# The order of ScalarE's two roundings in a down product, left to a planner or kept as written

## The chip, the cores and the metric

The kernel runs on one core of one Trainium2 chip. The metric is the device time of one execution in microseconds (us), the median of several runs. A profiled execution gives, beside its time, a record of every instruction on the core's engines: TensorE (PE for its matmuls, PEld for its weight loads), VectorE (DVE), ScalarE (ACT), GpSimd (POOL), SyncE (SP), and the DMA engines.

## The reference

One layer of an encoder on a sequence of 1024 frames of width 1024 in float32: a norm, a projection, two kinds of attention, gates and an output projection, then a feed-forward block of width 4096, and a last norm. The change touches the second matrix of the feed-forward block, `w_down`:

```python
h2 = rms_norm(x, norm2[l])
x = x + jnp.square(jax.nn.relu(h2 @ w_up[l])) @ w_down[l]
return rms_norm(x, final_norm)
```

## The kernel before, in words

All matrices are kept transposed, with features on the 128 partitions. A float32 product is made of three faster ones: each operand a is rounded to a_h (a type that TensorE reads at full rate), and a_l = a - a_h is rounded too; the product is w_h x_h + w_h x_l + w_l x_h. A rounding is a ScalarE copy (`CAST` in the profile), the subtraction runs on GpSimd for weights (`wl`) and on VectorE for activations (`xl`).

The large products go by a Strassen scheme: seven products of half size in place of eight. For the down product these are, in order, (weight, activation): (A11, B11), (S1, T1), (S2, T2), (S3, T3), (S4, B22), (A12, B21), (A22, T4). The activations B and T, 16 blocks of 128 x 512 for each product, were written to a DRAM array (`a_dram`) by the up product just before. The weights A are loaded from `wall`; the S are sums made on VectorE from blocks that stay in SBUF (`ka` and `ks`, 16 blocks each) and blocks that come in (`wr`, four buffers). S1 takes two loaded blocks a step, S3 one, S2 none, S4 one that is loaded into `ka`.

The stage has 7 x 16 = 112 steps. Step s takes one activation block and one weight block and issues 12 matmuls of 128 x 128 by 128 x 512: four output blocks m, three matmuls each. Four PSUM banks collect a product over its 16 steps; the other four are used by the next product. `prepare(s)` is written LEAD = 3 steps ahead of the matmuls of step s. It issues, in this order:

1. the load of the activation block (`xr`, six buffers);
2. its rounding `x..h` on ScalarE (line 1013; `xq` has XB = 4 buffers for each half);
3. the subtraction `x..l` on VectorE;
4. the loads and the VectorE sum of the weight of step s + WLEAD, that is two steps further on (`weight`, line 916);
5. the rounding `wh` of this step's own weight on ScalarE (line 165, in `split_w`; HL = 6 buffers), and the subtraction `wl` on GpSimd (line 167).

This written order is not by itself the order in an engine's queue. The program is laid out by a planner which simulates the kernel and puts, on each engine, an instruction ahead of another when it takes its inputs to be there sooner. `keep_in_program_order` takes that freedom from one instruction: it comes behind the instruction that was written last before it on the same engine, whatever that is, a DMA issue included. The class `Ordered` applies it to all calls made through it. Before the change the stage does so for VectorE's subtractions and sums (`VO`), for the loads on SyncE (`LO`) and for the last matmuls (`TO`); ScalarE and GpSimd are left to the planner, and so is all of `between`.

`between(n, banks)` takes a finished product out of PSUM, a piece after each step of the next product: a ScalarE copy after A11, VectorE totals after the others, after S2 and S3 also DMAs that add the residual from `x2_dram` (issued by GpSimd), and `final` (a square with its sum, and a scaling) for tiles that are complete. After S4 the norm of one half of the output is made and stored during A12, by `finish`: it stores in turn from SyncE and from ScalarE. The last product ends with the other half's norm. The other helpers are named in the profile's rows by line: L218 is the matmul of `product`, L96 any call through `Ordered`, L941 the residual's DMA, L233 and L948 the square and the scaling of `final`, L957 and L964 to L967 the norm and the stores of `finish`.

Of the kernel before, what the change touches and what calls it, by code (L numbers as in the profile page):

```python
# [82 lines left out]
def hybrid_block(ctx: ExitStack, tc: tile.TileContext, xT, g1, wall, wf, fb, relb, relt, rows, g2, g3, outT):  # L83
    nc = tc.nc
    V, A, G, T = nc.vector, nc.scalar, nc.gpsimd, nc.tensor
# [9 lines left out]
        def __getattr__(self, name):  # L95
            return lambda *a, **kw: tc.keep_in_program_order(getattr(self.eng, name)(*a, **kw))  # L96

    VO, TO, LO = Ordered(V), Ordered(T), Ordered(nc.sync)
    load_r = nc.gpsimd.dma_start

    def pool(stack, name, side, bufs=1, **kw):
# [10 lines left out]
    def tmp(name, dt=F32):  # L112
        return tp.tile([P, HALF], dt, tag="t", name=name, bufs=8)
# [9 lines left out]
    for n, (step, cm) in enumerate(((-1, 1), (1, -1))):  # L123
        m = cpool.tile([P, 3, P], F32R, tag=f"mask{n}", name=f"mask{n}")
        raw = tmp("raw")[:, 0:3 * P].rearrange("p (n q) -> p n q", q=P)
# [34 lines left out]
        load(q, wall[u, :, n, :])  # L160
        return q

    def split_w(src, name):
        wh = wp.tile([P, HALF], F32R, tag="wh", name=f"wh_{name}", bufs=HL)
        A.copy(wh, src)  # L165
        wl = wp.tile([P, HALF], F32R, tag="wl", name=f"wl_{name}", bufs=HL)
        G.tensor_tensor(wl, src, wh.bitcast(F32), op=ALU.subtract)  # L167
        return wh.rearrange("p (k m) -> p k m", m=P), wl.rearrange("p (k m) -> p k m", m=P)

    def plain_w(u, c):  # L170

        parts = [split_w(quarter(u, n), f"{u}_{n}") for n in ((0, 1), (3, 2))[c]]
        return [(parts[k // 4][0][:, k % 4, :], parts[k // 4][1][:, k % 4, :]) for k in range(KC)]

    def strassen_w(u, sum_eng, want=ALL):
# [20 lines left out]
        for name in want:  # L196
            if name in ("A11", "A12", "A22"):
                src = raw(int(name == "A12") + 2 * int(name == "A22"))
            elif name in ("S1", "S2"):
                if "S2" in want:  # L200
                    total("S2")
                src = total(name)
            elif name == "S3":
                src = raw(3)
                G.tensor_tensor(src, raw(0), src, op=ALU.subtract)
            else:
                src = total("S2")
                G.tensor_tensor(src, raw(1), src, op=ALU.subtract)
            out[name] = split_w(src, f"{u}_{name}")
# [102 lines left out]
    for h in range(2):  # L312
# [3 lines left out]
        for n, k in enumerate(PAIRED if h else range(KC)):  # L316
            xg = etile(f"xg{k}") if h == 0 else tmp(f"xg{k}")
            load(xg, xT[:, k, hs(h)])
            sum_squares(xg, n == 0, rstd[:, hs(h)], G if h else V)
            V.tensor_scalar(xg, xg, gt[:, 0, k:k + 1], None, op0=ALU.mult)  # L320
            split(xk(k, h), xg, V)
            blocks[k, h] = xg
            first, last = n == 0, n == KC - 1
            for c, ps in enumerate(banks):
                if (c, k // 4) not in ew:
                    ew[c, k // 4] = split_w(quarter(U_GATE + c // 2, ((0, 1), (3, 2))[c % 2][k // 4]), f"g{c}_{k}")
                w = [t[:, k % 4, :] for t in ew[c, k // 4]]
                for wi, xi in ((0, 0), (0, 1), (1, 0)):
                    T.matmul(ps, w[wi], xk(k, h)[xi], start=(first and wi + xi == 0), stop=(last and wi == 1),
                             skip_group_check=True)  # L330
            if h == 0 and first:
                for i, g in ((1, g2), (2, g3)):
                    load(gt[:, i, :], g)
                wr = tmp("wfr")[:, 0:KC * NH].rearrange("p (k m) -> p k m", m=NH)
                load(wr, wf)
                w40 = tmp("w40", F32R)[:, 0:KC * 40].rearrange("p (k m) -> p k m", m=40)
                V.memset(w40.bitcast(F32), 0.0)
                V.tensor_copy(w40[:, :, 0:NH], wr)
                V.tensor_tensor(w40[:, :, 32:40], wr, w40[:, :, 0:NH].bitcast(F32), op=ALU.subtract)
            for t in range(2):  # L340
                T.matmul(pf[0:40, :], w40[:, k, :], xk(k, h)[t], start=(first and t == 0), stop=(last and t == 1),
                         skip_group_check=True)
            if h == 1 and k >= 4:
                combine(k - 4, blocks[k - 4, 0], blocks[k - 4, 1], blocks[k, 0], blocks[k, 1], (V, G))
# [571 lines left out]
    def weight(n, k, vec, ld):  # L916

        u = U_DOWN + k
        if n in ("A11", "S4"):
            ld(hold("a", k), wall[u, :, int(n == "S4"), :])  # L920
        if n in ("A11", "A12"):
            return held["a", k]
        if n == "A22":
            return quarter(u, 2, ld)
        if n == "S1":
            vec.tensor_tensor(hold("s", k), quarter(u, 3, ld), quarter(u, 2, ld), op=ALU.add)
        elif n == "S2":
            vec.tensor_tensor(held["s", k], held["s", k], held["a", k], op=ALU.subtract)
        elif n == "S3":
            vec.tensor_tensor(held["a", k], held["a", k], quarter(u, 3, ld), op=ALU.subtract)  # L930
            return held["a", k]
        else:
            vec.tensor_tensor(held["s", k], held["a", k], held["s", k], op=ALU.subtract)
        return held["s", k]
# [73 lines left out]
    def prepare(s):  # L1008
        _, n, x, k = steps[s]
        raw = xr.tile([P, HALF], F32, tag="xr", name=f"x{x}{k}", bufs=XR)  # L1010
        (load_r if s < GSTEPS else LO.dma_start)(raw, a_dram[XI[x], k])
        xs = tuple(xq.tile([P, HALF], F32R, tag="x" + t, name=f"x{x}{t}{k}", bufs=XB) for t in "hl")
        A.copy(xs[0], raw)  # L1013
        VO.tensor_tensor(xs[1], raw, xs[0].bitcast(F32), op=ALU.subtract)
        while len(summed) < min(s + WLEAD + 1, len(steps)):
            n_, k_ = steps[len(summed)][1::2]
            summed.append(weight(n_, k_, VO, load_r if len(summed) < GSTEPS else LO.dma_start))
        wh, wl = split_w(summed[s], f"{n}_{k}")
        return xs, wh, wl

    summed = []
    steps = [(i, n, x, k) for i, (n, x) in enumerate(STEPS) for k in range(16)]
    ready, rest = [], iter(())
    for s, (i, n, x, k) in enumerate(steps):
        while len(ready) < min(s + LEAD + 1, len(steps)):
            ready.append(prepare(len(ready)))
        if k == 0:
            banks = [psm[i % 2].tile([P, HALF], F32, tag="d", name=f"d{n}_{m}") for m in range(4)]

        def multiply(m, k):  # L1030
            xs, wh, wl = ready[16 * i + k]
            product(banks[m], k == 0, [((wh[:, m, :], wl[:, m, :]), xs)], k < 15,
                    TO if n == "A22" and k >= 12 - STAG else T)

        if n == "A22" and k == 15 - STAG:

            for _ in rest:
                pass
            rest = between(n, banks)
            for m in range(4):  # L1040
                for k in range(15 - STAG, 16):
                    multiply(m, k)
                next(rest)
            break
        for m in range(4):
            multiply(m, k)
        if k:
            next(rest, None)
        if k == 15:
            for _ in rest:  # L1050
                pass
            rest = between(n, banks)
# [64 lines left out]
```

## Time and profile before

| what | value |
|---|---|
| time, median of 3 runs | 1573.29 us (1568.55 to 1576.57) |
| time of the profiled execution | 1575.07 us |
| its span, first to last instruction | 1573.3 us |
| mean granted TensorE clock | 0.977 |
| TensorE matmuls, busy | 1479.9 us, 94% |
| VectorE, busy | 1020.3 us, 65% |
| GpSimd, busy | 918.7 us, 58% |
| ScalarE, busy | 733.7 us, 47% |
| down product, first matmul to end of the span | 1221.8 to 1573.3 us |

In the rows shown below a line stands for one instruction or a group of them: its start in us from the span's beginning or its count, its duration, engine and line, what it writes and reads (`wh_S<-ks` is the rounding of a weight sum, `xT2l<-xT,xT2h` the subtraction for an activation of T2), and in brackets how long the engine stood idle before it and what ended that. Matmuls overlap each other, so distances between starts say more than their durations.

### The profile page before, as it was taken

How to read it: one execution, taken by the hardware profiler on the slowest of the kernel's cores; microseconds unless marked ns; L12 is line 12 of the kernel's file. 1: busy time of each engine (PE TensorE's matmuls, PEld its weight loads, DVE VectorE, ACT ScalarE, POOL GpSimd, SP SyncE). 2: the span in 40 equal slices, each digit the busy share in tenths (PEclk: the TensorE clock that was granted, in tenths of full speed). 3: DMA queues.
4: the chain of work that ended last, by engine and by line, in shares of the span. 5: the costliest groups of instructions: out<-in, count | busy, mean ns of one | idle time of the engine just before them, and what ended most of it. 6: DMA issues, size and time to landing. Idle time of an engine off the chain costs nothing.

```text
span 1573.3 us, 21039 instructions
## 1 busy us (share of the span) xinstructions
PE 1479.9 (94%) x6788; PEld 1207.7 (77%) x6788; DVE 1020.3 (65%) x1543; ACT 733.7 (47%) x1379; POOL 918.7 (58%) x735
## 2 busy tenths in 40 slices
PE   7698999999969989999999999999999899998996
PEld 4486888888848878888777888888888787676785
DVE  8989565654446778766424686666666656667764
ACT  5543333344228877656525543333333443333652
POOL 6886787869752222221086478788875634446661
PEclk9899999999979999999999999999999999999998
DMA  4155667773495897875466424444444674478362
GB/s 151 52 148 134 189 188 203 215 222 119 155 213 138 170 195 175 199 198 143 150 200 205 153 83 169 155 149 154 148 154 174 221 237 138 137 217 215 108 225 84
DMA packets 150320, 262.92 MB, mean 167 GB/s; under 512 B 21880, under 2 KB 39544, under 8 KB 147072
## 3 DMA queue, kind: packets, MB, share of 16 engines
q1 hardware_dynamic: 75968, 136.79, 28.6%
q10 hardware_dynamic: 50304, 84.24, 16.7%
q0 software_dynamic: 23936, 40.54, 11.9%
q8 instruction: 53, 0.87, 0.2%
q14 instruction: 59, 0.48, 0.1%
HBM read 175.19 MB, written 86.31 MB: 166 GB/s over the span
## 4 chain that ended last, share of the span: by engine, by line
PE 32%; issue 6%; POOL 4%; DVE 4%; DMA 4%; ACT 2%; SPq 0%; DVEq 0%; ACTq 0%; POOLq 0%
PE u L218 18%; PE dA L218 6%; PE o L218 4%; POOL wl_S L167 2%; DMA xT<-a_dram 2%; DVE ks L96 1%; PE m L218 1%; PE dA L96 1%; POOL m L785 1%; PE dS L218 1%; POOL ml L269 1%; ACT xB22h L1013 0%; DMA accw<-x_dram 0%; DMA wr<-wall 0%; DMA rb<-r_dram 0%
## 5 line engine op out<-in xcount | busy, mean ns | idle before, releaser
L167 POOL TENSOR_TENSOR wl_A<-wr,wh_A 128x512 fp32r<-128x512 f32 x121 | 174.0, 1446 | 56.9 <-ACT wh_A L165 49.8
L167 POOL TENSOR_TENSOR wl_S<-S,wh_S 128x512 fp32r<-128x512 f32 x105 | 147.2, 1406 | 36.9 <-ACT wh_S L165 34.9
L165 ACT CAST wh_A<-wr 128x512 fp32r<-128x512 f32 x121 | 75.0, 620 | 114.1 <-DMA a_dram<-at 52.5
L269 DVE TENSOR_TENSOR tl<-p,th 128x512 fp32r<-128x512 f32 (+1 forms) x192 | 108.3, 586 | 28.1 <-ACT th L268 23.3
L167 POOL TENSOR_TENSOR wl_S<-ks,wh_S 128x512 fp32r<-128x512 f32 x48 | 62.9, 1334 | 82.4 <-ACT wh_S L165 78.7
L165 ACT CAST wh_S<-S 128x512 fp32r<-128x512 f32 x105 | 64.0, 618 | 78.6 <-PE u L218 41.2
L268 ACT CAST th<-p 128x512 fp32r<-128x512 f32 (+1 forms) x192 | 92.4, 509 | 9.8 <-PE pv L702 4.4
L458 DVE CUSTOM_DVE_ANT_0 s<-s,bc 128x384 f32<-128x384 f32 (+3 forms) x128 | 69.7, 561 | 36.4 <-PE s L451 19.6
L451 PE MATMUL s<-qk 128*128 128x384 f32 (+2 forms) x192 | 63.7, 364 | 25.9 <-DMA qk<-qk_dram 14.6
L519 DVE TENSOR_TENSOR cc<-u,u 128x512 f32<-128x512 f32 x70 | 47.9, 686 | 55.6 <-PE u L218 55.3
L188 POOL TENSOR_TENSOR S<-wr,wr 128x512 f32<-128x512 f32 x36 | 51.1, 1420 | 48.0 <-DMA wr<-wall 36.3
L165 ACT CAST wh_S<-ks 128x512 fp32r<-128x512 f32 x48 | 29.7, 621 | 92.2 <-DVE ks L96 92.2
L686 PE MATMUL st<-sk 82*128 82x512 f32 (+1 forms) x192 | 66.4, 347 | 0.7 <-DMA sk<-m_rows 0.7
L678 PE MATMUL st<-qk 128*128 128x512 f32 (+1 forms) x192 | 66.8, 352 | 0.0
L701 PE MATMUL pv<-th,v 128*128 128x512 f32 (+1 forms) x192 | 65.5, 341 | 1.1 <-ACT on L714 0.6
L880 ACT ACTIVATE v<-v 128x512 f32<-128x512 f32 x64 | 40.4, 632 | 55.6 <-DVE v L879 55.6
L167 POOL TENSOR_TENSOR wl_A<-ka,wh_A 128x512 fp32r<-128x512 f32 x32 | 48.8, 1542 | 29.3 <-ACT wh_A L165 29.2
L703 PE MATMUL pv<-tl,v 128*128 128x512 f32 (+1 forms) x192 | 65.0, 338 | 0.1
L702 PE MATMUL pv<-th,v 128*64 128x512 f32 (+1 forms) x192 | 65.0, 338 | 0.0
L268 ACT CAST qkh<-qk 128x512 fp32r<-128x512 f32 x32 | 19.9, 622 | 96.6 <-DMA qk_dram<-qkl 38.1
L698 ACT ACTIVATE p<-st,ncq 128x512 f32<-128x512 f32 (+1 forms) x96 | 54.1, 598 | 20.6 <-PE st L694 14.1
L451 PEld LDWEIGHTS s<-qk 128*128 128x128 f32 x192 | 36.6, 201 | 34.8 <-issue 8.3
(377 smaller groups left out, 5106.7 us busy)
## 6 DMA issues: line engine op xcount, KB each, us to landing
wr<-wall SPq DMA_DIRECT2D x243, 256.0 KB
qk<-qk_dram POOLq DMA_DIRECT2D x16, 1024.0 KB, 7.5
a_dram<-at ACTq DMA_DIRECT2D x64, 256.0 KB
xT<-a_dram SPq DMA_DIRECT2D x64, 256.0 KB
qk_dram<-qkh ACTq DMA_DIRECT2D x96, 128.0 KB
a_dram<-v ACTq DMA_DIRECT2D x48, 256.0 KB
xB<-a_dram SPq DMA_DIRECT2D x44, 256.0 KB
z_dram<-zt ACTq DMA_DIRECT2D x32, 256.0 KB
```

What stands on the lines that cost most here:

```text
L165: A.copy(wh, src)
L167: G.tensor_tensor(wl, src, wh.bitcast(F32), op=ALU.subtract)
L218: eng.matmul(bank, w[wi], x[xi], start=(first and t == 0), stop=(t == n - 1 and not part), skip_group_check=part or not first)
L268: A.copy(dst[0], src)
L269: eng.tensor_tensor(dst[1], src, dst[0].bitcast(F32), op=ALU.subtract)
L451: T.matmul(ps[:, :n], qk[:, 1, i * P:(i + 1) * P], qk[:, 0, ks:ks + n], start=True, stop=not diag)
L458: V.tensor_tensor_reduce(ps[:, :v], ps[:, :v], bc[:, b0:b0 + v], 1.0, prev, ALU.add, ALU.min, out)
L678: T.matmul(ps[:, c], qk[:, 0, keys], qk[:, 1, qs], start=True, stop=False)
L686: T.matmul(ps[:, c], sk[:, 0, keys], sk[:, 1, qs], start=False, stop=not extra)
L701: T.matmul(pv[:, c], v3[hh][:, j, 1:3, :], th[:, c], start=first, stop=False)
L702: T.matmul(pv[0:HD, c], v3[hh][:, j, 0, :], th[:, c], start=False, stop=False)
L703: T.matmul(pv[:, c], v3[hh][:, j, 1:3, :], tl[:, c], start=False, stop=last)
```

## The change

The two roundings of a step are issued through `Ordered(A)`: ScalarE's queue keeps them in the order in which `prepare` writes them, the activation's first, then the weight's, step by step, and each behind whatever ScalarE instruction was written last before it. `split_w` gets the engine as an argument; its other callers keep the free one. Nothing else changes: the same instructions, buffers and transfers.

```diff
-    VO, TO, LO = Ordered(V), Ordered(T), Ordered(nc.sync)
+    VO, TO, AO, LO = Ordered(V), Ordered(T), Ordered(A), Ordered(nc.sync)
...
-    def split_w(src, name):
+    def split_w(src, name, act=A):
         wh = wp.tile([P, HALF], F32R, tag="wh", name=f"wh_{name}", bufs=HL)
-        A.copy(wh, src)
+        act.copy(wh, src)
...
-        A.copy(xs[0], raw)
+        AO.copy(xs[0], raw)
         VO.tensor_tensor(xs[1], raw, xs[0].bitcast(F32), op=ALU.subtract)
...
-        wh, wl = split_w(summed[s], f"{n}_{k}")
+        wh, wl = split_w(summed[s], f"{n}_{k}", AO)
```

## The prediction, made before the change was run

> **What bounds the kernel now.** First the page's busy times: TensorE is the bound of the whole, and in the down product too, but not all the way.
>
> ```profile
> PE 1479.9 (94%) x6788; PEld 1207.7 (77%) x6788; DVE 1020.3 (65%) x1543; ACT 733.7 (47%) x1379; POOL 918.7 (58%) x735
> ```
>
> Then, for the last stage, the rows of line 218 (the matmuls), one group for each of the seven products; "first and last start" give where a product begins, and the next product's begin is its end.
>
> ```profile
> L218 PE MATMUL dA<-xB11h,wh_A x64: 389/389/628, 1221.8 to 1269.4; 128*128 128x512 f32 x64
> L218 PE MATMUL dS<-xT1h,wh_S x64: 387/389/396, 1270.1 to 1315.0; 128*128 128x512 f32 x64
> L218 PE MATMUL dS<-xT2h,wh_S x64: 387/389/397, 1315.6 to 1365.0; 128*128 128x512 f32 x64
> L218 PE MATMUL dS<-xT3h,wh_S x64: 387/389/397, 1365.6 to 1415.3; 128*128 128x512 f32 x64
> L218 PE MATMUL dS<-xB22h,wh_S x64: 387/389/397, 1415.9 to 1467.3; 128*128 128x512 f32 x64
> L218 PE MATMUL dA<-xB21h,wh_A x64: 388/389/486, 1468.0 to 1512.8; 128*128 128x512 f32 x64
> L218 PE MATMUL dA<-xT4h,wh_A x40: 389/389/389, 1513.5 to 1540.0; 128*128 128x512 f32 x40
> ```
>
> The last row gives the undisturbed pace: 40 matmuls of one kind, with two others between each pair, in 1540.0 - 1513.5 = 26.5 us, so 26.5 / 117 = 0.2265 us each, 2.72 us for a step of 12 and 43.5 us for a product of 192. The products took 48.3 (A11), 45.5 (S1), 50.0 (S2), 50.3 (S3), 52.1 (S4) and 45.5 us (A12). Over 43.5 that is 4.8, 2.0, 6.5, 6.8, 8.6 and 2.0 us. The 4.8 is the beginning of the stage and is taken up below; the other five sum to 25.9 us, the whole pot of this change.
>
> Third, who waits for whom in S1 to S4 (engine, line, waited for: us, times, longest):
>
> ```profile
> ACT wh_S L165 <- DVE ks L96: 84.7, 41, 6.6
> ACT wh_S L165 <- DVE ka L96: 32.0, 16, 3.7
> DVE xT2l L96 <- ACT xT2h L1013: 17.1, 14, 1.3
> PEld dS L218 <- DVE xT2l L96: 7.8, 13, 0.6
> ```
>
> ScalarE waits for VectorE in 57 of 64 steps, VectorE for ScalarE, and TensorE's weight loads at the end of that. The fourth view, the timeline of one step of S2, shows the ring:
>
> ```profile
> 1343.46 0.68 DVE L96 TENSOR_TENSOR ks<-ks,ka 128x512 f32<-128x512 f32 x1
> 1344.23 0.62 ACT L165 CAST wh_S<-ks 128x512 fp32r<-128x512 f32 x1 [2.09 <-DVE ks L96]
> 1344.76 0.62 ACT L1013 CAST xT2h<-xT 128x512 fp32r<-128x512 f32 x1
> 1344.93 1.29 POOL L167 TENSOR_TENSOR wl_S<-ks,wh_S 128x512 fp32r<-128x512 f32 x1 [1.93 <-ACT wh_S L165]
> 1345.41 1.36 DVE L96 TENSOR_TENSOR xT2l<-xT,xT2h 128x512 fp32r<-128x512 f32 x1 [1.27 <-ACT xT2h L1013]
> 1346.69 0.68 DVE L96 TENSOR_TENSOR ks<-ks,ka 128x512 f32<-128x512 f32 x1
> 1347.45 0.62 ACT L165 CAST wh_S<-ks 128x512 fp32r<-128x512 f32 x1 [2.08 <-DVE ks L96]
> ```
>
> VectorE makes the weight sum ks; ScalarE, first in its queue, rounds that sum (wh_S, 0.77 us after ks began); behind it stands the activation's rounding xT2h (0.53 later); xT2l on VectorE waits for that (0.65) and, behind xT2l in VectorE's fixed order, comes the next ks (1.28). 0.77 + 0.53 + 0.65 + 1.28 = 3.23 us, the distance of the two ks and of the two wh_S. Nobody is busy that long: it is latency around a ring. The sum that follows xl(s) belongs to step s+2 (WLEAD = 2). Its rounding stands ahead of x(s+1) and x(s+2), though no matmul needs it before step s+2; that place alone closes the ring within one step.
>
> **The change part by part.**
>
> *The two pinned roundings.* No instruction is added or removed; 224 roundings get a fixed place, each behind the ScalarE instruction written before it. A step's queue is now x(s), wh(s), x(s+1), wh(s+1), and so on. wh(s+2) then stands behind x(s+2), and the ring, x(s), xl(s), sum, wh(s+2), x(s+3), closes over three steps: 3.23 us of latency per three steps, 1.08 us each. The next bound per step is TensorE's 2.72, against ScalarE 2 x 0.52 = 1.04, GpSimd 1.29, and VectorE 1.36 + 0.68 = 2.04.
>
> *What then sets x(s).* It needs one of XB = 4 buffers, free when TensorE ends step s-4, three steps or 8.16 us before it starts s. Rounding 0.53, wh 0.62, wl 1.29 and some hand-offs are 2.5 us, rounding and xl 2.0 us. So the operands stand ready 5.6 us ahead where today they are late. This cover absorbs S1 to S3: of their 2.0 + 6.5 + 6.8 = 15.3 us I leave 0.5. Bounds: 0 and 15.3 left; 0.5 because A11's steps, whose ScalarE order has no weight sum in it, run at 2.72 already. What would be late next is S1's weights, two loads and an activation a step:
>
> ```profile
> 1283.00:1302.00 19.00, 19.00 (x85) 15.73 (x84) 11.42 (x13) 6.86 (x12) 7.39 (x7) 1.00 0.79 246
> 1513.50:1540.00 26.50, 26.50 (x119) 21.94 (x117) 18.32 (x18) 17.81 (x31) 16.92 (x12) 1.00 0.86 291
> 1272.43 4.19 DMA xT<-a_dram
> ```
>
> (Rows of the windows: after the five engines' busy times come clock, DMA share, GB/s; the last row is from the chain.) At 2.72 us S1 asks for 246 x 3.23 / 2.72 = 292 GB/s. A22 moved 291 while TensorE was busy in all its 26.50 us, so the rate can be had. The four raw buffers (two to a sum) give a load two steps, 5.44 us, against 4.19 to land and 0.68 for the sum: 0.57 is left for issuing. Were landing to grow with the rate, 4.19 x 292 / 246 = 4.97, a step would take some 2.83, 1.8 us too much over S1, inside the 5.6 of cover. 0 on the path.
>
> *S4, where GpSimd issues twelve residual transfers.* They aren't pinned and stay.
>
> ```profile
> 1422.32 0.89 POOL L941 DMA_DIRECT2D accw<-x_dram  x1
> 1424.98 1.64 POOL L167 TENSOR_TENSOR wl_S<-ks,wh_S 128x512 fp32r<-128x512 f32 x1
> 1426.24 1.23 POOL L941 DMA_DIRECT2D accw<-x_dram  x1
> 1434.71 5.32 POOL L167 TENSOR_TENSOR wl_S<-ks,wh_S 128x512 fp32r<-128x512 f32 x4
> 1434.75 5.84 DVE L96 TENSOR_TENSOR ks<-ka,ks 128x512 f32<-128x512 f32 x1
> 1427.71 0.63 ACT L233 ACTIVATE sq<-accw 128x512 f32<-128x512 f32 x1 [3.48 <-DMA accw<-x_dram]
> ```
>
> From 1422.3 to 1434.7 GpSimd makes one wl. Say a wl ended just before: the next ends 4.3 us later (in time), the one after 14.1 us later (12.4 + 0.4 + 1.3), and TensorE wants it 5.6 + 2 x 2.72 = 11.0 after: 3.1 us of wait. Meanwhile ScalarE stands 3.48 us before the square of accw (unpinned, waits for its transfer), within the cover; the four wl in a row stretch a VectorE sum to 5.84 us, about the whole cover, so 0.4 more. I leave 3.5 of 8.6 us. Bounds: 0 (the planner slips a wl between the issues) and 8.6.
>
> *A12.* Eight `final` pairs run here, one to a step: a square (0.63 above) and a scaling:
>
> ```profile
> 1474.41 0.71 ACT L948 ACTIVATE accw<-accw,gt 128x512 f32<-128x512 f32 x1
> ```
>
> With two roundings at 0.53, ScalarE has 2.4 of 2.72 us, and the pinned roundings queue behind each pair. The norm's matmuls and VectorE's sums stay as they are. I leave 1.5 of 2.0; bounds 0 and 5.1 (all eight pairs in one block, less the cover: 8 x 1.34 - 5.6).
>
> *The beginning.* The first pinned x stands behind the last ScalarE instruction of the up product, the store of the last difference (1224.23); today the first x roundings run ahead of it.
>
> ```profile
> 1221.78 1.75 PE L218 MATMUL dA<-xB11h,wh_A 128*128 128x512 f32 x4 [1.85 <-ACT wh_A L165]
> 1224.12 8.53 DVE L96 TENSOR_TENSOR xB11l<-xB,xB11h 128x512 fp32r<-128x512 f32 x5
> 1224.23 0.33 ACTq L888 DMA_DIRECT2D a_dram<-at  x1
> 1225.93 0.80 PE L218 MATMUL dA<-xB11l,wh_A 128*128 128x512 f32 x1 [2.40 <-DVE xB11l L96]
> 1225.00:1227.00 2.00, 1.07 (x3) 0.89 (x4) 2.00 (x2) 1.33 (x3) 2.00 (x3) 0.50 0.72 170
> ```
>
> x(0) runs from about 1224.7, wh(0) ends near 1225.85, and TensorE starts there instead of at 1221.78. But today it does only four matmuls (1.75 us) and then waits until 1225.93 for xl(0), whose place on VectorE behind the last difference doesn't change. So four matmuls are lost: 0.9 us at full clock, 1.75 at the 0.50 the windows grant there; I take 1.2. Bounds: -0.6 (ScalarE is rid of a 0.6 us rounding ahead of the last squares) and 4.1 (the whole shift). The Trainium skill, "TensorE: Matmul & The Clock Gate", section "What's actually happening", says that some 3.4 us without work halve the clock and 3.4 us of work restore it; by it the longer gap would shift the half-clock stretch and cost up to 1.7 us. The 0.50 right after today's gap agrees with it.
>
> *A22.* Its first weight, rounded early today at 1498.97, now stands behind x(0) of A22, which waits for its transfer.
>
> ```profile
> 1498.97 0.62 ACT L165 CAST wh_A<-wr 128x512 fp32r<-128x512 f32 x1 [1.67 <-POOL wl_A L167]
> 1505.23 0.34 SPq L967 DMA_DIRECT2D outT<-accv  x1
> 1508.86 0.62 ACT L1013 CAST xT4h<-xT 128x512 fp32r<-128x512 f32 x1 [4.38 <-DMA xT<-a_dram]
> ```
>
> SP's queue keeps its order: that load is behind the output store at 1505.23, which follows the norm. x lands by 1508.86, wh ends at 1510.0, wl by 1511.4, TensorE begins at 1513.5: 2.1 us to spare, so 0. Were the cover gone, wl would be late by what the load slips beyond 2.1 us.
>
> *The sum.* -25.9 + 0.5 + 3.5 + 1.5 + 1.2 = -19.2 us. The profiled execution took 1575.07 us (span 1573.3): 1555.9. The median shown is 1.8 lower, 1573.29, which would give 1554.1. I say 1555.
>
> **The rivals.**
>
> *Slower: VectorE becomes the bound.* One mechanism: each xl and each sum meets a GpSimd subtraction.
>
> ```profile
> 1379.74 1.78 DVE L96 TENSOR_TENSOR xT3l<-xT,xT3h 128x512 fp32r<-128x512 f32 x1
> 1381.44 1.77 DVE L96 TENSOR_TENSOR ka<-ka,wr 128x512 f32<-128x512 f32 x1
> ```
>
> Here they did: 3.55 us a step. Sixty-four such steps less the 5.6 of cover are 221.6 us, against 197.9 now: +23.7, 1599 us. It decides from 2.72 us a step. Against it: that was GpSimd catching up with several wl in a row; with one wl a step only one of the two meets it, 1.78 + 0.68 = 2.46. Chance 0.05.
>
> *VectorE and GpSimd never together.* Two VectorE operations of 0.68 and a wl of 1.29 are 2.65 us a step; totals of earlier products come on top, four in S2, eight in S3 and in S4:
>
> ```profile
> 1420.21 0.68 DVE L975 TENSOR_TENSOR accw<-dS,accv 128x512 f32<-128x512 f32 x1
> ```
>
> That makes 45.1, 47.8 and 47.8 us for these products, 10.2 over three times 43.5, less the cover of 5.6: 4.6, 1560 to 1561 with the rest as in the sum. For it: xl takes 1.36 beside wl, while the like sum ks takes 0.68. Against: the totals, which read PSUM, may run beside GpSimd. The Trainium skill, "SBUF — State Buffer", "Who interferes with whom", states it as a rule: a tensor_tensor with both inputs in SBUF and a GpSimd read block one another wholly. The 1.36 agrees. *Late loads in S1* end alike: from 5.5 us of landing the cover is used up; at 6.0 a step takes (6.0 + 0.68) / 2 = 3.34, and S1 loses 16 x 0.62 - 5.6 = 4.3 us: 1560. A22's row speaks against. Both with S4 and A12 at their upper bounds (5.1 and 3.6 more) reach 1567 and beyond. Chances 0.12 for the first and 0.08 for the loads, 1561 to 1567.
>
> *No change.* TensorE's release of the x buffers, not the queue, might hold the roundings; then 1575, and S1 to S4 stay. Against: x follows wh at 0.53 us in each step, and the wait is put down to ks. Chance 0.08.
>
> **How the numbers follow.** Forecast 0.62, 1549 (S4's and A12's rest at 0, less the beginning) to 1561; better than that 0.05; the two limits 0.20; no change 0.08; slower 0.05. Range 1549 to 1567 for 0.82. About 0.5%, 7.9 us, is what a measurement of this kernel can tell from none: faster 0.85 (all but the end of the limits), same 0.10, slower 0.05.
>
> **What would show it.** Right: S1, S2 and S3 near 43.5 us each; wh_S no longer waiting for ks; xl ready before TensorE; ks done a step or more before its rounding; S4 near 47; the first matmul of the stage near 1226; the tail from the last matmul unchanged. Wrong: if S1 stays over 46 with ks waiting for loads, if VectorE is busy throughout S2 and S3, if S4's wl wait exceeds 6 us, or if the planner, with these roundings fixed, moves the unpinned work of other engines.

## The result and the profile after

The changed kernel takes 1554.5 us in the median (1549.6 to 1556.94, 4 runs) against 1574.93 (1568.55 to 1584.64, 4 runs) for the kernel before on the same chip: a ratio of 0.9858, interval 0.9827 to 0.9889. That is 1.4% faster, and half a microsecond from the forecast of 1555.0. The profiled execution took 1553.71 us, 21.4 less than the one before, with a span of 1551.9 us and a mean granted clock of 0.976.

The page first: busy time of the engines, and the chain that ended last by engine.

```profile
PE 1469.4 (95%) x6788; PEld 1212.7 (78%) x6788; DVE 1018.2 (66%) x1543; ACT 735.3 (47%) x1379; POOL 919.3 (59%) x735
PE 40%; POOL 3%; DMA 3%; DVE 2%; issue 2%; ACT 1%; SPq 0%; ACTq 0%; DVEq 0%; POOLq 0%
```

The work is what it was: ScalarE's 1379 and VectorE's 1543 instructions are unchanged in number. On the chain, TensorE's share is now 40%, where it was 32%; engines and DMAs that it waited for hold 3% or less each. In S1 to S4 the chain is TensorE alone, 174.32 us without a break.

The rows of line 218, one for each product, as before the change:

```profile
L218 PE MATMUL dA<-xB11h,wh_A x64: 389/389/795, 1226.4 to 1271.2; 128*128 128x512 f32 x64
L218 PE MATMUL dS<-xT1h,wh_S x64: 389/389/390, 1271.9 to 1314.7; 128*128 128x512 f32 x64
L218 PE MATMUL dS<-xT2h,wh_S x64: 388/389/390, 1315.4 to 1358.3; 128*128 128x512 f32 x64
L218 PE MATMUL dS<-xT3h,wh_S x64: 389/389/390, 1358.9 to 1401.8; 128*128 128x512 f32 x64
L218 PE MATMUL dS<-xB22h,wh_S x64: 389/389/393, 1402.5 to 1445.5; 128*128 128x512 f32 x64
L218 PE MATMUL dA<-xB21h,wh_A x64: 387/389/486, 1446.2 to 1489.7; 128*128 128x512 f32 x64
L218 PE MATMUL dA<-xT4h,wh_A x40: 389/389/449, 1490.8 to 1518.3; 128*128 128x512 f32 x40
```

From the begin of one product to the begin of the next (two decimals are from the instructions themselves; A22 ends one matmul's pace, 0.23 us, after its last matmul's start):

| us | A11 | S1 | S2 | S3 | S4 | A12 | A22 | last matmul's start to the end |
|---|---|---|---|---|---|---|---|---|
| before | 48.31 | 45.56 | 50.0 | 50.3 | 52.05 | 45.48 | 43.52 | 16.5 |
| after | 45.51 | 43.52 | 43.52 | 43.52 | 43.76 | 44.57 | 44.98 | 16.4 |

S1, S2 and S3 run at 43.52 us, which is the undisturbed pace of 16 x 2.72, and S4 is 0.24 above it. These four alone went from 197.9 to 174.3 us, 23.6 less. The stage begins 4.6 us later (1226.4 for 1221.8), and A11 gives 2.8 of them back.

Who waits for whom, from 1200 us on (engine, line, waited for: us, times, longest):

```profile
ACT wh_S L96 <- DVE ks L96: 6.5, 6, 2.5
ACT wh_S L96 <- DVE ka L96: 4.1, 3, 2.2
ACT xT1h L96 <- DMA xT<-a_dram: 19.9, 12, 2.5
PE dA L218 <- ACT wh_A L96: 5.5, 1, 5.5
```

ScalarE's wait for the sums, over the same stretch of the kernel before, was 92.2 and 32.0 us (the prediction's 84.7 is for a shorter one, from 1270 us to 1468); it is 6.5 and 4.1 (its rounding now carries line 96, since it goes through `Ordered`). The only wait for an operand that is listed for the products' matmuls in the stage is the last row, its first one; their weight loads have two short ones more, 0.4 and 0.5 us for a wl. One step of S2 in the timeline, all but TensorE:

```profile
1342.87 0.62 ACT L96 CAST xT2h<-xT 128x512 fp32r<-128x512 f32 x1 [1.58 <-issue]
1343.39 0.61 ACT L96 CAST wh_S<-ks 128x512 fp32r<-128x512 f32 x1
1343.52 0.69 DVE L96 TENSOR_TENSOR xT2l<-xT,xT2h 128x512 fp32r<-128x512 f32 x1 [0.33 <-ACT xT2h L96]
1344.08 1.28 POOL L167 TENSOR_TENSOR wl_S<-ks,wh_S 128x512 fp32r<-128x512 f32 x1 [1.44 <-ACT wh_S L96]
1344.13 1.78 DVE L96 TENSOR_TENSOR ks<-ks,ka 128x512 f32<-128x512 f32 x1
1345.59 0.62 ACT L96 CAST xT2h<-xT 128x512 fp32r<-128x512 f32 x1 [1.58 <-issue]
```

ScalarE rounds x, then the weight at once: that sum was made long before, so it does not wait for it. At `issue` the profile names nothing that the engine waited for; here x begins 0.08 us after the last matmul of the step four before it ends (1342.79), as its four buffers ask. VectorE's xT2l follows its rounding, and the next sum follows that; the two roundings of x are 2.72 us apart, TensorE's pace, where the weight's were 3.23. The ring is open.

### The profile page after: what moved, and what is told of

Its sections match the earlier page's. It is cut to its first block, busy times and chain, and to the rows that moved or that the text cites. A ratio compares the mean times of both kernels' runs of the same rounds, so it can differ in the third digit from the quotient of the medians.

```text
span 1551.9 us, 21027 instructions
## 1 busy us (share of the span) xinstructions
PE 1469.4 (95%) x6788; PEld 1212.7 (78%) x6788; DVE 1018.2 (66%) x1543; ACT 735.3 (47%) x1379; POOL 919.3 (59%) x735
## 4 chain that ended last, share of the span: by engine, by line
PE 40%; POOL 3%; DMA 3%; DVE 2%; issue 2%; ACT 1%; SPq 0%; ACTq 0%; DVEq 0%; POOLq 0%
PE u L218 19%; PE dS L218 11%; PE dA L218 5%; PE o L218 4%; POOL wl_A L167 1%; POOL m L785 1%; POOL ml L269 1%; DMA xT<-a_dram 1%; DMA z<-z_dram 1%; PE dA L96 0%; DMA wr<-wall 0%; DMA rb<-r_dram 0%; DVE B22l L269 0%; DVE T2l L269 0%; DMA r_dram<-d 0%
## 5 line engine op out<-in xcount | busy, mean ns | idle before, releaser
L165 ACT CAST wh_A<-wr 128x512 fp32r<-128x512 f32 x105 | 65.1, 620 | 103.0 <-DMA a_dram<-at 52.5
L167 POOL TENSOR_TENSOR wl_S<-ks,wh_S 128x512 fp32r<-128x512 f32 x48 | 68.7, 1512 | 53.8 <-ACT wh_S L96 53.8
L167 POOL TENSOR_TENSOR wl_A<-ka,wh_A 128x512 fp32r<-128x512 f32 x32 | 45.2, 1422 | 47.1 <-ACT wh_A L96 47.1
L208 POOL TENSOR_TENSOR S<-wr,S 128x512 f32<-128x512 f32 x35 | 49.6, 1418 | 17.8 <-DMA wr<-wall 14.3
```

The lines of the kernel that those rows point to most:

```text
L165: act.copy(wh, src)
```

## The experiments

Each edit is made in the changed kernel. All were compared with the kernel before; its median was 1576.76 us (15 runs) beside the first four below and 1576.09 (9 runs) beside the last three. The product durations, worked out as above:

| us | A11 | S1 | S2 | S3 | S4 | A12 | A22 |
|---|---|---|---|---|---|---|---|
| only x in order | 45.38 | 45.56 | 50.0 | 50.29 | 52.27 | 45.48 | 43.53 |
| only wh in order | 48.23 | 43.52 | 43.52 | 43.52 | 43.77 | 45.48 | 43.9 |
| no weight lead | 45.23 | 46.95 | 51.09 | 54.38 | 58.07 | 44.57 | 45.35 |
| weight lead of one | 45.55 | 43.52 | 43.52 | 43.52 | 44.66 | 44.57 | 44.56 |
| three x buffers | 45.19 | 43.52 | 43.63 | 45.64 | 50.47 | 45.31 | 45.49 |
| S4's matmuls as written | 45.53 | 43.52 | 43.52 | 43.52 | 45.13 | 44.57 | 44.43 |
| ends not pinned | 48.96 | 43.52 | 43.52 | 43.52 | 43.79 | 44.57 | 45.03 |

My theory: the gain comes from the place of the weight's rounding, which closes the ring through ScalarE's queue. The rivals: that the activation's place counts, or only their sum; and that the cover in buffers is not what keeps S2 to S4 at TensorE's pace.

**Only x in order.**

```diff
-        wh, wl = split_w(summed[s], f"{n}_{k}", AO)
+        wh, wl = split_w(summed[s], f"{n}_{k}")
```

> Only the activations' roundings are pinned, each behind the ScalarE instruction written before it; the weights' roundings are free again. Theory (the ring): nothing then keeps wh(s+2) from going ahead of x(s+1), so the ring of VectorE's sum, wh, x, xl closes within one step as before: S1 to S4 at 3.23 us a step where TensorE has used up its lead, about 198 us for the four products, 1573 us or a little less, within 0.5% of the kernel before. Rival (the activations' place is what counts: they come first, and the gain is theirs): S1 to S4 near 174 us, 1554.

Measured: 1575.38 us, ratio 0.9993 (0.9972 to 1.0014; 10 runs). No change. S1 to S4 take 198.1 us, as before, and the old wait is back in the view of the waits (first row), 92.4 us where the kernel before has 92.2; the second row is S2's group of matmuls:

```profile
ACT wh_S L165 <- DVE ks L96: 92.4, 45, 6.8
L218 PE MATMUL dS<-xT2h,wh_S x64: 387/389/396, 1321.3 to 1370.6; 128*128 128x512 f32 x64
```

**Only wh in order.**

```diff
-        AO.copy(xs[0], raw)
+        A.copy(xs[0], raw)
```

> Only the weights' roundings are pinned, the activations' are free. Since wh(s) is written right behind x(s), each wh still stands behind its own x. Theory (the ring): it is open, S1 to S4 near 174 us, about 1554 us, the whole gain; the first roundings of the stage may again run ahead of the up product's end, up to 1 us better. Rival (the activations' place counts): most of the gain is gone, 1565 to 1573.

Measured: 1553.8 us, ratio 0.9845 (0.9809 to 0.9882). The whole gain, with S1 to S4 at 174.3 us; the same two rows:

```profile
ACT wh_S L96 <- DVE ks L96: 8.4, 9, 2.5
L218 PE MATMUL dS<-xT2h,wh_S x64: 389/389/389, 1312.0 to 1354.8; 128*128 128x512 f32 x64
```

The two together show which half works: keeping the weight's rounding behind its own step's activation. The activation's pin adds nothing that can be measured.

**No weight lead.** Both pins stay; the sum of step s is made in step s, so the ring closes within one step again although nothing is out of its written order.

```diff
-WLEAD = 2
+WLEAD = 0
```

> The changed kernel with WLEAD = 0: VectorE makes the weight sum of step s itself behind xl(s), not that of step s+2. Both roundings stay pinned. Theory: the ring x(s), xl(s), sum, wh(s), x(s+1) closes within one step again, 3.23 us, although ScalarE keeps the written order: S1 to S4 take 4 x 16 x 3.23 less the 5.6 us of lead, about 201 us against 174, so about 1581 us (1574 to 1590), no faster than the kernel before. Rival (the written order of the two roundings is by itself what helps, e.g. by its order on GpSimd and TensorE): 1554 to 1560.

Measured: 1591.56 us, ratio 1.0079 (1.0051 to 1.0107), slower than the kernel before. The timeline in S2:

```profile
1341.17 0.68 DVE L96 TENSOR_TENSOR ks<-ks,ka 128x512 f32<-128x512 f32 x1
1341.93 0.62 ACT L96 CAST wh_S<-ks 128x512 fp32r<-128x512 f32 x1 [2.09 <-DVE ks L96]
1342.46 0.62 ACT L96 CAST xT2h<-xT 128x512 fp32r<-128x512 f32 x1
1343.11 1.36 DVE L96 TENSOR_TENSOR xT2l<-xT,xT2h 128x512 fp32r<-128x512 f32 x1 [1.26 <-ACT xT2h L96]
1344.39 0.68 DVE L96 TENSOR_TENSOR ks<-ks,ka 128x512 f32<-128x512 f32 x1
1345.16 0.62 ACT L96 CAST wh_S<-ks 128x512 fp32r<-128x512 f32 x1 [2.08 <-DVE ks L96]
```

Sum, rounding of the weight, rounding of x, xl, next sum: 1344.39 - 1341.17 = 3.22 us, the ring of the kernel before within a hundredth, and again with xl at 1.36 beside wl. S2 takes 51.09, about 16 of these. The direction and the ring were as expected, the size was not: S3 and S4 take 54.4 and 58.1 us. With no lead at all the totals add to the ring, where the expectation let the ring cover them: in S4 eight of them stand between two sums ks on VectorE, 1427.80 and 1433.79, which is 5.99 us for 3.22. The issues of the residual fall there too; their share was not taken apart. So the length of the ring in steps decides, not the written order as such.

**A weight lead of one.** `WLEAD = 1`, the ring over two steps: 3.23 / 2 = 1.6 us a step, below 2.72.

> The changed kernel with WLEAD = 1. Theory: the ring closes over two steps, 3.23 / 2 = 1.6 us a step, still under TensorE's 2.72: S1 to S4 near 174 us and 1554 us as with 2, at most 3 us more where the loads of S1 have less lead. Rival (each step of lead of the sums is worth the same): half way between the changed kernel and WLEAD = 0, some 1567.

Measured: 1558.3 us (1551.0 to 1565.94), ratio 0.9876 (0.9826 to 0.9926). S1 to S3 are at 43.52, S4 loses 0.9 more than with a lead of two; the time can't be told from the change's. The ring over two steps is short enough.

**Three x buffers.** This takes one step of the cover that the prediction worked out, 5.6 - 2.7 = 2.9 us left.

```diff
-LEAD, XB, XR = 3, 4, 6
+LEAD, XB, XR = 3, 3, 6
```

> The changed kernel with three buffers for rounded activations (XB = 3) in place of four. Theory: an operand is ready one step of TensorE less ahead, 2.9 us in place of 5.6, and the delays that the lead hid come out: S1's late loads 1 us, the block of eight totals in S3 2, GpSimd's residual transfers in S4 2 to 3, A12 and A22 1 to 3 each: about 8 us, 1562 (1557 to 1568). Rival (the open ring alone is the gain and the lead isn't needed): 1554.

Measured: 1563.29 us, ratio 0.9919 (0.9884 to 0.9954). The total is as expected, the split is not: S1 loses nothing, S3 2.1 us and S4 6.7. The view of the waits names an xl in S3 and a wl in S4, for 1.8 and 3.9 us of that:

```profile
PE dS L218 <- POOL wl_S L167: 3.9, 1, 3.9
PE dS L218 <- DVE xT3l L96: 1.8, 1, 1.8
```

About 9 us of S2 to S4, then, are held by the fourth buffer. The cover that is left is more than the 2.9 us of the sum: in S2 of this run an undisturbed xl ends 4.3 us ahead of its first matmul. S1's late loads take that down to 0.8 us at S1's last step, but not to nothing.

**S4's matmuls as written.** In the changed kernel the planner put the four matmuls with the late wl at the end of their step. Here they are held in the written order (`TO`, as in A22's end).

```diff
-                    TO if n == "A22" and k >= 12 - STAG else T)
+                    TO if n == "S4" or n == "A22" and k >= 12 - STAG else T)
```

> The changed kernel with TensorE's matmuls of S4 in the written order (per block m: wh xh, wh xl, wl xh); today the planner puts the four matmuls with wl last in the step that wl reaches late. Theory: that order is what hid 1.8 us of the wait for wl behind GpSimd's residual transfers, so S4 takes 45.5 us in place of 43.8, and 1 to 2 us go on the time, too little for the runs, but seen in the trace. Rival (the wl slipped between the transfers alone did it): S4 stays at 43.8.

Measured: 1554.31 us, ratio 0.985 (0.9811 to 0.989): the time cannot tell the two apart, but the trace can. S4 takes 45.13 us, 1.37 more, and in the timeline TensorE waits for wl once:

```profile
1409.77 2.15 POOL L167 TENSOR_TENSOR wl_S<-ks,wh_S 128x512 fp32r<-128x512 f32 x1
1411.98 0.50 PE L96 MATMUL dS<-xB22h,wl_S 128*128 128x512 f32 x1 [1.31 <-POOL wl_S L167]
```

**Ends not pinned.** A11's first four steps and A22 get ScalarE's free order back.

```diff
-        AO.copy(xs[0], raw)
+        act = A if s < 4 or n == "A22" else AO
+        act.copy(xs[0], raw)
...
-        wh, wl = split_w(summed[s], f"{n}_{k}", AO)
+        wh, wl = split_w(summed[s], f"{n}_{k}", act)
```

> The changed kernel with the roundings of the first four steps and of all of A22 left to the planner, and those between pinned. Theory: the first matmul of the stage comes 4 us earlier and the stage's beginning costs 0.8 us less; A12 and A22 together take 89.0 us as before the change in place of 89.6: 1553, not to be told from 1554.5 by the runs, but by the trace. Rival (the roundings of A22 pinned cost more than the trace shows, or the freed ones fall into another bad order): 1548 or 1558.

Measured: 1555.33 us (1548.53 to 1561.9), ratio 0.9857 (0.9804 to 0.991), the same as the change. The first matmul again comes early with a wait behind it (A11 48.96), and the beginning, from the last sum of the up product to the end of A11, takes 50.2 us for the change's 50.4, so 0.2 less and not the expected 0.8. A12 with A22 takes 44.57 + 45.03 = 89.60 us, not the 89.0 that was expected. The order of A22's roundings is thus not what costs the half microsecond there.

## Why the prediction was right

Term by term, between the two profiled executions:

| term | predicted | measured |
|---|---|---|
| S1 to S3 | -14.8 | -15.3 |
| S4 | -5.1 | -8.3 |
| A12 and A22 | -0.5 | +0.55 |
| beginning | +1.2 | +0.84 |
| stage's start, from execution to execution | 0 | +0.96 |
| tail | 0 | -0.14 |
| sum | -19.2 | -21.4 |

The mechanism was as predicted; that the median lies half a microsecond from the forecast is in part luck. S4 came out 3.2 us better than told, A12 with A22 and the stage's start 2.0 us worse, and single executions spread over 7 us (after) and 16 us (before). The stage's start is put down to the execution: in the profiled executions of the seven experiments, none of which edits the up product, its last sum starts between 1218.1 and 1227.0 us (1220.6 before, 1221.5 after).

*The ring* stood as told: 3.23 us, closed by the place of wh(s+2). Only wh in order opens it, only x in order leaves it, and no lead closes it anew.

*The cover* was slightly larger than worked out. In the step of S2 shown above, xT2l ends at 1344.21 and the first matmul that reads it starts at 1351.01, 6.8 us later; wl ends at 1345.36 and its first matmul starts at 1351.24, 5.9 us later. The prediction had 8.16 - 2.0 = 6.1 us for xl and 5.6 for wl, and used 5.6 for both. VectorE and GpSimd need not keep pace from step to step, only within these; with three buffers they no longer do.

*S1's loads* became the last to arrive, as the prediction named them, though it put the weights' first: ScalarE waits for the activations', VectorE's sums for the weights' as well (12.7 us in 14 steps). ScalarE's roundings of x there (the first and the last of ten that wait for their transfer), and the window over them:

```profile
1278.51 0.62 ACT L96 CAST xT1h<-xT 128x512 fp32r<-128x512 f32 x1 [2.25 <-DMA xT<-a_dram]
1305.12 0.62 ACT L96 CAST xT1h<-xT 128x512 fp32r<-128x512 f32 x1 [1.62 <-DMA xT<-a_dram]
1278.00:1305.00 27.00, 27.00 (x121) 22.34 (x120) 13.98 (x19) 10.29 (x18) 11.59 (x9) 1.00 0.86 271
```

Nine periods in 26.61 us are 2.96 us each, at 271 GB/s. The estimate was 2.83, so the loads are a little slower than told. The lead of xl over its first matmul shrinks accordingly in these nine steps, from 5.9 to 3.7 us (9 x 0.24 = 2.2); that lies inside the cover, and S1 shows none of it.

*S4* is the mis-sized term: 3.5 us were left over, and 0.24 is what it cost. The prediction put one wl before the twelve issues are over, the next 14.1 us after the last one ahead of them, and TensorE's need at 11.0. The timeline of the changed kernel there, GpSimd, then VectorE, then TensorE:

```profile
1401.20 1.28 POOL L167 TENSOR_TENSOR wl_S<-ks,wh_S 128x512 fp32r<-128x512 f32 x1 [1.44 <-ACT wh_S L96]
1405.10 1.64 POOL L167 TENSOR_TENSOR wl_S<-ks,wh_S 128x512 fp32r<-128x512 f32 x1
1412.80 2.41 POOL L167 TENSOR_TENSOR wl_S<-ks,wh_S 128x512 fp32r<-128x512 f32 x1
1414.96 6.14 POOL L167 TENSOR_TENSOR wl_S<-ks,wh_S 128x512 fp32r<-128x512 f32 x4
1414.20 7.46 DVE L96 TENSOR_TENSOR xB22l<-xB,xB22h 128x512 fp32r<-128x512 f32 x1 [1.42 <-ACT xB22h L96]
1414.93 0.39 PE L218 MATMUL dS<-xB22l,wh_S 128*128 128x512 f32 x1
1415.27 1.20 PE L218 MATMUL dS<-xB22h,wl_S 128*128 128x512 f32 x4
1416.30 0.39 PE L218 MATMUL dS<-xB22h,wh_S 128*128 128x512 f32 x1
```

The wl before the issues ended at 1402.48, one came at 1405.10 as predicted, and the planner slipped the next between two issues at 1412.80: it ended at 1415.21, 12.7 us after the first, not 14.1. And the four matmuls that use it stand last in their step, in one group, so that their deadline was later too. TensorE's starts are 0.34 and 1.03 us apart around the group, 0.11 us late before it and 0.12 behind it (the pace for four is 0.91). With the written order S4 takes 1.37 us more. So of the 3.1 us of predicted wait 1.4 went because the wl came 1.4 us sooner, another 1.4 by the order of TensorE's own queue, and 0.3 is what remains. "The planner slips a wl between the issues" was the lower bound of the term; it should have been weighed with TensorE's free order. VectorE's delay stayed within the cover, but barely: its xB22l took 7.46 us beside the wl of 1412.80 and the four after it, 6.8 more than alone, and ended 0.3 us before its first matmul (1421.97). By the 5.6 us of the prediction it would have been 1.2 us late, for which 0.4 was put down. The prediction had also named as a sign of being wrong that the planner moves unpinned work of other engines; it did so here, on GpSimd and TensorE, and it helped.

*A12 and A22.* Together 89.00 before and 89.55 after. The 0.5 that the prediction took from A12 was not there to be had: the 2.0 us that A12 stood over 43.5 were no wait for an operand of its own (the view of the waits lists none there for its matmuls or weight loads), but 16 small matmuls of the norm that run inside it, before the change and after. That A12 gained 0.9 and A22 lost 1.46 is a matter of the order at their border: the weight part of A12's last step comes late, and A22's first matmuls run ahead of it. The matmuls of A12 with wl, as a group, and the timeline at the border:

```profile
L218 PE MATMUL dA<-xB21h,wl_A x64: 388/389/397, 1446.7 to 1493.3; 128*128 128x512 f32 x64
1484.85 3.01 POOL L964 TENSOR_TENSOR accw<-accw,rstd 128x512 f32<-128x512 f32 x2
1487.83 1.73 POOL L167 TENSOR_TENSOR wl_A<-ka,wh_A 128x512 fp32r<-128x512 f32 x1
1486.70 0.62 ACT L96 CAST xT4h<-xT 128x512 fp32r<-128x512 f32 x1 [3.42 <-POOL accw L964]
```

GpSimd multiplies two output tiles (line 964) up to 1487.86, and wl follows; A12's wl matmuls end at 1493.3, after A22's first (1490.8). A22's zero was argued from the weight standing behind x(0); x(0) came at 1486.70 and that was early enough. Most of the half microsecond is one wait in A22: at 1529.25 a weight load of line 96 has waited 0.5 us for a wl, and the two matmuls there start 0.39 us late in sum. It is not the order of A22's roundings, since with the ends not pinned it is an xl that is waited for in A22 instead, 0.7 us, and the sum is 89.60; with S4 as written no such wait is listed, and the sum is 89.00 as before the change (89.38 with only wh in order, 89.13 with a lead of one). In the changed kernel nine roundings of x in A22 wait for their transfer, 15.0 us in all, where before the change one did, 4.4 us; but with S4 as written nine wait as well, 11.2 us, so that alone does not cost it. Why an operand is late in one of these kernels and in time in another stays open.

*The beginning.* ScalarE's queue is the predicted one: store, x(0), wh(0), then TensorE. The timeline of the changed kernel, and three windows (five engines' busy time, clock, DMA share, GB/s):

```profile
1224.83 0.33 ACTq L888 DMA_DIRECT2D a_dram<-at  x1
1225.20 0.62 ACT L96 CAST xB11h<-xB 128x512 fp32r<-128x512 f32 x1 [1.12 <-DVE at L887]
1225.73 0.61 ACT L96 CAST wh_A<-ka 128x512 fp32r<-128x512 f32 x1
1226.39 1.22 PE L218 MATMUL dA<-xB11h,wh_A 128*128 128x512 f32 x2 [5.51 <-ACT wh_A L96]
1226.40:1228.40 2.00, 2.00 (x5) 1.61 (x6) 1.65 (x3) 2.00 (x5) 1.98 (x2) 0.50 0.86 221
1228.40:1230.40 2.00, 2.00 (x7) 1.52 (x6) 2.00 (x2) 1.06 (x3) 2.00 (x2) 0.50 0.88 313
1230.40:1240.00 9.60, 9.60 (x44) 7.94 (x43) 4.02 (x4) 3.96 (x8) 6.68 (x5) 1.00 0.88 295
```

From the last sum of the up product to the end of A11 it takes 50.4 us where it took 49.5, +0.84 against +1.2. In the window rows the clock is 0.50 for 4.0 us behind a gap of 5.51 us, then 1.00. The Trainium skill, "TensorE: Matmul & The Clock Gate", section "What's actually happening", has 3.4 us of work restore the clock; 4.0 us agree within the windows' width of 2 us. The other half of that rule is not shown here: the 0.50 before the change, which the prediction calls agreement, stood behind gaps of only 1.85 and 2.40 us with four matmuls between them. The gain of an early start was small either way: with the ends not pinned TensorE begins early and waits, and the time is the same.

*The rivals.* That VectorE would become the bound is refuted by S2 at 43.52. The nearer one, that VectorE and GpSimd never work together, had its mechanism half right. The timeline of the changed kernel in S3, GpSimd and VectorE:

```profile
1360.42 1.29 POOL L167 TENSOR_TENSOR wl_S<-ka,wh_S 128x512 fp32r<-128x512 f32 x1 [0.57 <-ACT wh_S L96]
1360.64 0.68 DVE L975 TENSOR_TENSOR accu<-dS,accp 128x512 f32<-128x512 f32 x1
1364.56 1.64 POOL L167 TENSOR_TENSOR wl_S<-ka,wh_S 128x512 fp32r<-128x512 f32 x1
1364.23 2.53 DVE L96 TENSOR_TENSOR xT3l<-xT,xT3h 128x512 fp32r<-128x512 f32 x1
```

xT3l, with both inputs in SBUF, ends at 1366.76, 0.56 us after the wl beside it (1366.20), although its record begins 0.33 us before that of the wl. The sum ks in S2 ends 0.55 after its wl (1345.91 and 1345.36), and S4's xB22l of 7.46 us ends 0.56 after the last of four (1421.66 and 1421.10): in these three places VectorE waited for GpSimd. But the total accu, which reads PSUM, takes its usual 0.68 although a wl runs beside it from begin to end (1360.42 to 1361.71). So the totals do not add to the 2.65 us a step that the two take one after the other, and 2.65 is below 2.72. The Trainium skill, "SBUF — State Buffer", section "Who interferes with whom", says both: a VectorE instruction with two SBUF inputs contends with a GpSimd instruction that reads SBUF, and one with at most one SBUF input, outside the two-port modes, does not. These rows agree.

## What to carry to other kernels

When no engine is full and all wait in turn, follow one step until it bites its own tail: add the latencies around the ring and count over how many steps it closes. A result that is made ahead for a later step must not have its consumer placed ahead of nearer work in an in-order queue; here the pin of that one instruction was worth 23 us, and pinning its neighbour nothing. Then count the cover in buffers, since that says which bursts (issues, VectorE and GpSimd in each other's way, late loads) may still happen without cost.

## What was not expected of the hardware

A VectorE subtraction of 0.69 us was stretched to 7.46 us by back-to-back GpSimd subtractions: it began 0.76 us before four that followed each other, got in between none of them, and ended 0.56 us behind the last. In S2 the longer of a step's two VectorE operations was the one that began just behind a wl: xl with 1.36 (the sum 0.68) before, the sum with 1.78 (xl 0.69) after, with the same instructions. Between GpSimd's residual issues a wl took 1.64 and 2.41 us for its 1.28.
